# The dt projection of a hybrid decoder layer: plain fp32 with four 32-column blocks side by side, over an input summed on VectorE

## The chip, the core and the metric

The kernel runs on one core of a Trainium2 chip. The metric is the time of one execution on the device in microseconds (us). The engines are named as in the profile: PE is TensorE's matrix multiply and PEld its weight load, DVE is VectorE, ACT is ScalarE, POOL is GpSimd, and SP issues most of the transfers. Each engine takes its instructions in the order in which the program lists them.

## What is computed

One layer of a hybrid decoder is applied to 1024 prompt rows and to 64 sample rows (8 sequences of 8). Both go through one input projection, which is here the part that matters:

```python
h = _rmsnorm(x, norm_pre)
proj = jnp.einsum('bld,de->ble', h, w_in)
z, xbc, dt_raw, u, g, gates = jnp.split(proj, IN_OFFSETS, axis=-1)
...
dt = jax.nn.softplus(dt_raw.astype(F32) + dt_bias.astype(F32))
a = -jnp.exp(a_log.astype(F32))
y, new_ssm = _ssd(xs, dt, a, bm, cm, ssm_state.astype(F32))
```

`dt_raw` has one column for each of 16 heads. From dt follow the decays of a chunked scan (`_ssd`). The remaining columns of the projection go through a causal convolution, a pooling branch and gates, then through two branch projections and one output projection. All inputs and outputs are fp32.

## The kernel before

The 1088 rows lie along the free dimension as columns. The normalised input stands transposed in SBUF as a pair, `Hhi` and `Hlo`, each of 8 slices (k) of 128 partitions by 1088 columns: `Hhi` is the value rounded to the matmul's reduced fp32 type (fp32r) and `Hlo` the rest. Weights are split in the same way into `whi` and `wlo`. A 128-column piece of a projection is the work of `group3` (L143): for each of three column chunks (`CHUNKS`: 384, 384 and 320 columns), 8 slices times 3 products, `Hhi`*`whi`, `Hlo`*`whi` and `Hhi`*`wlo`.

The order of all work is written by hand. `main` is a list of matmul groups, one for each slot of the program; `at(slot, fn, key=...)` puts other work behind a slot's matmuls, sorted by key, and `at_pe` puts PE work ahead of them. Slots 0 to 5 are the groups of the first two convolution pieces, slots 6 to 8 those of the third (`cv[8]`), slot 9 is the dt projection (`DtStep.group`), and slot 10 the next convolution piece. Behind each convolution group come its evacuation from PSUM (`evac`, ACT, L335 to L343, one slot later, key 0), three multiply-adds of the convolution (`taps`, DVE, L349, two slots later, key 5), and a tanh on ACT (L356) with a product on DVE (`fin`, L357 and L360, three slots later, key 1). While convolution pieces run, ACT rounds the weights of the next piece (L94) and POOL takes the rest (L95).

`DtStep` computes dt. `load` fetches the 16 weight columns into `dst` and clears `dsw`, `conv` splits them into two column groups of `dsw`, so that one product gives the high and the low part of the weight in different output rows. `group` runs 3 chunks times 8 slices times 2 products (L388). `evac` copies 32 output rows to SBUF (L410), `tok` turns them by nine transposes (L416) so that rows become partitions, and `softplus` adds the two halves (L424) and takes the softplus (L426 to L437). `cums` (L441 to L444) makes the running sums by four matmuls two slots later. A scratch pool `z` of 13 tiles of 128 x 1088 is handed out by `zt()` and given back by `zfree()`.

Further on, the sample rows use matmuls of plain fp32 whose outputs are 32 partitions high, four side by side by `tile_position=(0, 32 * c)` (L752).

Of the kernel before, what the change touches and what calls it, by code (L numbers as in the profile page):

```python
# [9 lines left out]
F32 = mybir.dt.float32  # L10
F32R = mybir.dt.float32r
I32 = mybir.dt.int32
AF = mybir.ActivationFunctionType
ALU = mybir.AluOpType
# [5 lines left out]
NS = DB * DS  # L20
LT = LP + NS
# [4 lines left out]
C_Z, C_X, C_B, C_C, C_DT, C_U, C_G, C_GA, C_GB = 0, 1024, 2048, 2304, 2560, 2576, 3088, 3600, 4624  # L26
# [12 lines left out]
def hybrid_decoder_step(  # L39
# [6 lines left out]
    nc = tc.nc  # L46
# [11 lines left out]
    def nm(s):  # L58
        uid[0] += 1
        return f"{s}_{uid[0]}"  # L60
# [4 lines left out]
    def zt(shape=(128, LT), dt=F32):  # L65
        for s in big:
            if s.free:
                s.free -= 1
                t = s.pool.tile(list(shape), dt, tag=s.tag, name=nm(s.tag))
                owner[id(t)] = (s, t)  # L70
                return t
        raise AssertionError("no slot is free")

    def zfree(*ts):
        for t in ts:
            owner.pop(id(t))[0].free += 1
# [7 lines left out]
    def ct(shape, name, dt=F32):  # L84
        return cst.tile(shape, dt, name=name)

    def bank(tag):
        return px.tile([128, 512], F32, tag=tag, name=nm(tag))
# [4 lines left out]
    def split(hi, lo, src, eng=None):  # L93
        nc.scalar.copy(hi, src)  # L94
        (eng or nc.vector).tensor_tensor(lo, src, hi.bitcast(F32), op=ALU.subtract)  # L95
# [6 lines left out]
    def at(slot, fn, *args, key=1):  # L102
        post[slot].append((key, len(post[slot]), fn, args))

    def at_pe(slot, fn, *args, first=False):
        pe[slot].insert(0 if first else len(pe[slot]), (fn, args))
# [8 lines left out]
    class Slab:  # L115
# [8 lines left out]
        def conv(self, eng=None):  # L124
            self.hi = wp.tile([128, 8, 128], F32R, tag="whi", name=nm("whi"))
            self.lo = wp.tile([128, 8, 128], F32R, tag="wlo", name=nm("wlo"))
            n = self.kn
            split(self.hi[:, 0:n], self.lo[:, 0:n], self.raw[:, 0:n], eng)
# [23 lines left out]
    ident = ct([128, 128], "ident")  # L152
# [6 lines left out]
    Hhi = hpool.tile([128, KD, LT], F32R, name="Hhi")  # L159
    Hlo = hpool.tile([128, KD, LT], F32R, name="Hlo")  # L160
# [9 lines left out]
    s1 = s0_ctx.__enter__()  # L170
# [127 lines left out]
    class Conv:  # L298
# [15 lines left out]
        def group(self, c):  # L314
            t, box = group3(self.slab, c, hrhs, self.ch)
            at(t + 1, self.evac, c, box, key=0)
            at(t + 2, self.taps, c, key=5)
            at(t + 3, self.fin, c, key=1)
            return t
# [49 lines left out]

    class DtStep:  # L370
        def load(self):
            self.raw = s1.tile([128, 8, 16], F32, tag="dst", name="dst")
            nc.sync.dma_start(self.raw, w_in[0].rearrange("(k p) e -> p k e", p=128)[:, :, C_DT:C_DT + 16])
            self.w = s1.tile([128, 8, 128], F32R, tag="dsw", name="dsw")
            nc.gpsimd.memset(self.w.bitcast(F32), 0.0)

        def conv(self):
            split(self.w[:, :, 0:16], self.w[:, :, 16:32], self.raw, nc.gpsimd)

        def group(self):  # L380
            box = {}

            def emit():
                for c, (a, b) in enumerate(CHUNKS):
                    ps = box[c] = bank(("m0", "pyo", "pyo")[c])
                    for k in range(8):
                        for p, h in enumerate((Hhi, Hlo)):
                            nc.tensor.matmul(ps[:, 0:b - a], self.w[:, k], h[:, k, a:b], start=k == 0 and p == 0,  # L388
                                             stop=k == 7 and p == 1)

            main.append(emit)
            t = len(main) - 1
            at(t + 1, self.evac, box, key=0)
            at_pe(t + 3, self.tok)
            at(t + 3, self.softplus)
            at_pe(t + 5, self.cums)
            at(t + 5, self.cums_post)
            at_pe(t + 6, self.rowsT)
            at(t + 6, self.rows_post, key=4)
            at(t + 7, self.store)  # L400
            at(t + 22, common_a, key=6)
            at(t + 25, common_b, key=6)
            at(t + 26, common_c, key=6)

        def evac(self, box):
            self.dtr = zt((32, LT))
            self.tmp = zt((128, 5, 9, 16))
            nc.gpsimd.memset(self.tmp[64:128, 0, 8], 0.0)
            for c, (a, b) in enumerate(CHUNKS):
                nc.scalar.copy(self.dtr[:, a:b], box[c][0:32, 0:b - a])  # L410

        def tok(self):
            self.pd = bank("pst")
            for t in range(9):
                n = 128 if t < 8 else NS
                nc.tensor.transpose(self.pd[0:n, 32 * t:32 * t + 32], self.dtr[:, 128 * t:128 * t + n], ident[0:32, 0:32])  # L416
            zfree(self.dtr)

        def softplus(self):
            v, tt, u, e, r = (self.tmp[:, i] for i in range(5))  # L420
            self.adt = v
            for n, t0, m in ((128, 0, 8), (NS, 8, 1)):
                d = v[0:n, t0:t0 + m]
                nc.vector.tensor_reduce(d, self.pd[0:n, 32 * t0:32 * t0 + 32 * m].rearrange("p (t i h) -> p t h i", t=m, i=2),  # L424
                                        axis=mybir.AxisListType.X, op=ALU.add)
                nc.vector.tensor_tensor(d, d, bias_b[0:n].unsqueeze(1).to_broadcast([n, m, 16]), op=ALU.add)  # L426
            nc.scalar.activation(tt, v, AF.Abs)
            nc.scalar.activation(tt, tt, AF.Exp, scale=-1.0)
            nc.vector.tensor_scalar(u, tt, 1.0, None, op0=ALU.add)
            nc.vector.tensor_scalar(e, u, 1.0, None, op0=ALU.subtract)  # L430
            nc.vector.tensor_tensor(e, tt, e, op=ALU.subtract)
            nc.vector.reciprocal(r, u)
            nc.vector.tensor_tensor(e, e, r, op=ALU.mult)
            nc.scalar.activation(u, u, AF.Ln)
            nc.vector.tensor_tensor(e, e, u, op=ALU.add)
            nc.vector.scalar_tensor_tensor(dtv, v, 0.0, e, op0=ALU.max, op1=ALU.add)
            nc.vector.tensor_tensor(v, dtv, na.unsqueeze(1).to_broadcast([128, 9, 16]), op=ALU.mult)  # L437
# [732 lines left out]
    for slot, part in enumerate(plan.split("|")):  # L1170
        for w in part.split():
            fn, n = steps[w[0]], int(w[1])
# [9 lines left out]
    at(0, cv[8].slab.dma, key=5)  # L1182
    dts = DtStep()
    at(3, dts.load, key=5)
    at(6, dts.conv, key=5)
    at(2, hist_dma, key=5)
    at(5, zfree, npre, key=9)

# [67 lines left out]
    for j in range(8):  # L1256
        pr = Pair(j)
        pr.tx = p4 - 1 + j // 4 * 7
        t = p4 + 1 + 2 * j
# [250 lines left out]
```

## Time and profile before

| | us |
|---|---|
| median of 3 runs | 894.23 (893.12 to 894.34) |
| the profiled execution: its time | 894.35 |
| its span (first to last instruction) | 892.6 |
| PE busy | 879.9 (99%) |
| PEld busy | 843.7 (95%) |
| DVE busy | 551.2 (62%) |
| ACT busy | 348.8 (39%) |
| POOL busy | 217.4 (24%) |

The time lies 1.75 us above the span. A row of the timeline gives start and duration of an instruction, or of several equal ones in a row, in us from the span's start, and in brackets how long the engine was idle ahead of it and what ended that. Matmuls overlap, so their durations add up to more than the time they take; what one takes in a stream is the distance between starts. A plain fp32 matmul has two rows, a matmul on fp32r operands one.

### The profile page before, as it was taken

How to read it: one execution, taken by the hardware profiler on the slowest of the kernel's cores; microseconds unless marked ns; L12 is line 12 of the kernel's file. 1: busy time of each engine (PE TensorE's matmuls, PEld its weight loads, DVE VectorE, ACT ScalarE, POOL GpSimd, SP SyncE). 2: the span in 40 equal slices, each digit the busy share in tenths (PEclk: the TensorE clock that was granted, in tenths of full speed). 3: DMA queues.
4: the chain of work that ended last, by engine and by line, in shares of the span. 5: the costliest groups of instructions: out<-in, count | busy, mean ns of one | idle time of the engine just before them, and what ended most of it. 6: DMA issues, size and time to landing. Idle time of an engine off the chain costs nothing.

```text
span 892.6 us, 14398 instructions
## 1 busy us (share of the span) xinstructions
PE 879.9 (99%) x5558; PEld 843.7 (95%) x5558; DVE 551.2 (62%) x999; ACT 348.8 (39%) x770; POOL 217.4 (24%) x297
## 2 busy tenths in 40 slices
PE   7999999999999999999999999999999999999997
PEld 5999999999999999999999999999999999988886
DVE  6776796989667765457746554357356627963322
ACT  6645565656375543345333141112333224331111
POOL 6332264756465652121100000000000000001101
PEclk9999999999999999999999999999999999999999
DMA  8010233342345335453311124433111123722322
GB/s 275 9 48 24 77 95 97 99 128 71 103 129 156 105 96 164 127 160 101 95 49 36 54 84 149 143 114 99 34 49 51 31 79 115 264 74 71 100 99 85
DMA packets 110322, 87.97 MB, mean 99 GB/s; under 512 B 8474, under 2 KB 97550, under 8 KB 110253
## 3 DMA queue, kind: packets, MB, share of 16 engines
q1 hardware_dynamic: 110109, 86.98, 32.5%
q8 instruction: 44, 0.72, 0.3%
q14 instruction: 25, 0.20, 0.1%
q10 hardware_dynamic: 144, 0.07, 0.0%
HBM read 69.46 MB, written 17.56 MB: 97 GB/s over the span
## 4 chain that ended last, share of the span: by engine, by line
PE 93%; DVE 1%; ACT 1%; POOL 1%; issue 0%; DVEq 0%; POOLq 0%; ACTq 0%
PE m L143 54%; PE pyo L143 16%; PE m L1399 3%; PE pyo L1399 3%; PE xb L1399 2%; PE pst L1399 2%; PE pyo L575 2%; PE pyo L582 2%; PE pst L586 1%; PE xb L711 1%; PE xb L542 1%; PE pyo L388 1%; DVE r L841 1%; PE pyo L752 1%; PE pst L759 0%
## 5 line engine op out<-in xcount | busy, mean ns | idle before, releaser
L143 PE MATMUL m<-Hhi,whi 128*128 128x384 f32 (+3 forms) x872 | 289.0, 331 | 0.0
L143 PE MATMUL m<-Hhi,wlo 128*128 128x384 f32 (+3 forms) x872 | 285.4, 327 | 0.0
L143 PE MATMUL m<-Hlo,whi 128*128 128x384 f32 (+3 forms) x872 | 285.3, 327 | 0.0
L143 PEld LDWEIGHTS m<-Hhi,whi 128*128 128x128 f32 x872 | 164.6, 189 | 0.6
L143 PEld LDWEIGHTS m<-Hlo,whi 128*128 128x128 f32 x872 | 164.6, 189 | 0.3
L143 PEld LDWEIGHTS m<-Hhi,wlo 128*128 128x128 f32 x872 | 164.4, 189 | 0.3
L349 DVE SCALAR_TENSOR_TENSOR r<-r,par,r 128x384 f32<-128x384 f32 (+3 forms) x108 | 94.6, 876 | 2.6
L94 ACT CAST whi<-raw 128x1024 fp32r<-128x1024 f32 (+1 forms) x67 | 59.8, 892 | 91.4 <-PE m L143 53.6
L95 DVE TENSOR_TENSOR wlo<-raw,whi 128x512 fp32r<-128x512 f32 (+1 forms) x46 | 43.4, 944 | 65.2 <-ACT whi L94 65.1
L95 POOL TENSOR_TENSOR wlo<-raw,whi 128x1024 fp32r<-128x1024 f32 x21 | 51.6, 2457 | 40.9 <-ACT whi L94 40.9
L143 PE MATMUL pyo<-Hhi,whi 128*128 128x384 f32 (+1 forms) x184 | 59.8, 325 | 0.0
L143 PE MATMUL pyo<-Hhi,wlo 128*128 128x384 f32 (+1 forms) x184 | 59.7, 325 | 0.0
L143 PE MATMUL pyo<-Hlo,whi 128*128 128x384 f32 (+1 forms) x184 | 59.7, 324 | 0.0
L143 PE MATMUL m<-z,whi 128*128 128x384 f32 (+1 forms) x217 | 54.0, 327 | 0.0
L143 PE MATMUL pyo<-z,whi 128*128 128x384 f32 (+1 forms) x191 | 47.7, 327 | 0.0
L568 POOL TENSOR_TENSOR sa<-sa,cb 128x512 f32<-128x512 f32 x28 | 39.8, 1441 | 3.7 <-ACT sa L564 3.7
L143 PEld LDWEIGHTS m<-z,whi 128*128 128x128 f32 x217 | 38.4, 188 | 0.0
L143 PE MATMUL m<-z,wlo 128*128 128x384 f32 (+1 forms) x115 | 37.6, 327 | 0.0
L563 ACT ACTIVATE sa<-sa,acm 128x128 f32<-128x128 f32 x112 | 35.6, 389 | 0.0
L609 DVE SCALAR_TENSOR_TENSOR z<-z,dsk,se 128x128 f32<-128x128 f32 x56 | 34.8, 660 | 1.0
L1434 POOL TENSOR_SCALAR t<-t 128x1 f32<-128x1 f32 (+1 forms) x9 | 2.5, 276 | 133.7 <-ACT q L1431 133.7
L143 PEld LDWEIGHTS pyo<-Hlo,whi 128*128 128x128 f32 x184 | 34.6, 188 | 0.0
(386 smaller groups left out, 1608.5 us busy)
## 6 DMA issues: line engine op xcount, KB each, us to landing
raw<-in_w_in_dram SPq DMA_DIRECT2D x43, 512.0 KB, 4.0
z<-in_x_prompt_dram SPq DMA_DIRECT2D x15, 512.0 KB, 4.5
sa<-dscr SPq DMA_DIRECT2D x28, 256.0 KB, 4.4
z<-spill SPq DMA_DIRECT2D x11, 544.0 KB, 5.1
raw<-in_w_branch_a_dram SPq DMA_DIRECT2D x16, 256.0 KB, 2.8
r<-in_w_out_dram SPq DMA_DIRECT2D x16, 256.0 KB, 4.4
se<-dscr SPq DMA_DIRECT2D x56, 64.0 KB, 3.8
out_dram<-q SPq DMA_DIRECT2D x14, 256.0 KB, 2.1
```

The source lines that it names most:

```text
L94: nc.scalar.copy(hi, src)
L95: (eng or nc.vector).tensor_tensor(lo, src, hi.bitcast(F32), op=ALU.subtract)
L143: nc.tensor.matmul(ps[:, 0:b - a], slab.w(k, p), rhs(k, p)[:, a:b], start=k == 0 and p == 0, stop=k == slab.kn - 1 and p == 2)
L349: nc.vector.scalar_tensor_tensor(A, R[:, k:k + w], cw(k, i), A, op0=ALU.mult, op1=ALU.add)
L388: nc.tensor.matmul(ps[:, 0:b - a], self.w[:, k], h[:, k, a:b], start=k == 0 and p == 0, stop=k == 7 and p == 1)
L542: nc.tensor.transpose(p[:, 128 * i:128 * i + 128], X[2 * self.u + i][:, self.cols], ident)
L563: nc.scalar.activation(A[:, h], A[:, h], AF.Relu, bias=acm[:, self.c, hh:hh + 1], scale=-1.0)
L568: nc.gpsimd.tensor_tensor(A, A, CBs[self.c, self.g].unsqueeze(1).to_broadcast([128, 4, 128]), op=ALU.mult)
L575: nc.tensor.matmul(py[64 * q:64 * q + 64, 128 * i:128 * i + 128], s.x0[:, 2 * i + q], s.A[:, 2 * i + q], start=True, stop=True)
L582: nc.tensor.matmul(py[:, 256 + 128 * i:384 + 128 * i], hs[:, 128 * i:128 * i + 128], Ct[self.g][:, self.cols], start=True, stop=True)
L609: nc.vector.scalar_tensor_tensor(xv, xv, dsk[:, j:j + 1], self.E[:, i] if self.c else py[:, 128 * i:128 * i + 128], op0=ALU.mult, op1=ALU.add)
L1399: nc.tensor.matmul(box["ps"][:, 0:b - a], lh, rh[k][:, a:b], start=kk == 0 and i == 0, stop=kk == 7 and rh is Wlo)
```

## The change

The high and low parts of the input are added on DVE, one slice at a time, into eight full fp32 tiles (`whole`, placed in slots 5 to 8, two in each slot, with key 9). The weight is kept in plain fp32, padded to 32 columns, and no longer split. The dt projection then runs as 24 plain fp32 matmuls: in each chunk, slices 0 to 3 go to the output partitions 0, 32, 64 and 96, and slices 4 to 7 are accumulated on them. The four partial sums are evacuated as 128 rows, transposed as full 128-row tiles into three PSUM banks, and added by the reduction in `softplus`, which now adds four parts and is made of three instructions.

```diff
--- before.py
+++ after.py
@@ -369,13 +369,15 @@
 
     class DtStep:
         def load(self):
-            self.raw = s1.tile([128, 8, 16], F32, tag="dst", name="dst")
-            nc.sync.dma_start(self.raw, w_in[0].rearrange("(k p) e -> p k e", p=128)[:, :, C_DT:C_DT + 16])
-            self.w = s1.tile([128, 8, 128], F32R, tag="dsw", name="dsw")
-            nc.gpsimd.memset(self.w.bitcast(F32), 0.0)
-
-        def conv(self):
-            split(self.w[:, :, 0:16], self.w[:, :, 16:32], self.raw, nc.gpsimd)
+            self.w = s1.tile([128, 8, 32], F32, tag="dsw", name="dsw")
+            nc.gpsimd.memset(self.w, 0.0)
+            nc.sync.dma_start(self.w[:, :, 0:16], w_in[0].rearrange("(k p) e -> p k e", p=128)[:, :, C_DT:C_DT + 16])
+
+        def whole(self, k):
+            if k == 0:
+                self.h = []
+            self.h.append(zt())
+            nc.vector.tensor_tensor(self.h[k], Hhi[:, k].bitcast(F32), Hlo[:, k].bitcast(F32), op=ALU.add)
 
         def group(self):
             box = {}
@@ -383,10 +385,12 @@
             def emit():
                 for c, (a, b) in enumerate(CHUNKS):
                     ps = box[c] = bank(("m0", "pyo", "pyo")[c])
-                    for k in range(8):
-                        for p, h in enumerate((Hhi, Hlo)):
-                            nc.tensor.matmul(ps[:, 0:b - a], self.w[:, k], h[:, k, a:b], start=k == 0 and p == 0,
-                                             stop=k == 7 and p == 1)
+                    for r in range(2):
+                        for g in range(4):
+                            k = 4 * r + g
+                            nc.tensor.matmul(ps[32 * g:32 * g + 32, 0:b - a], self.w[:, k], self.h[k][:, a:b], start=r == 0,
+                                             stop=r == 1, tile_position=(0, 32 * g))
+                zfree(*self.h)
 
             main.append(emit)
             t = len(main) - 1
@@ -403,26 +407,29 @@
             at(t + 26, common_c, key=6)
 
         def evac(self, box):
-            self.dtr = zt((32, LT))
+            self.dtr = zt()
             self.tmp = zt((128, 5, 9, 16))
             nc.gpsimd.memset(self.tmp[64:128, 0, 8], 0.0)
             for c, (a, b) in enumerate(CHUNKS):
-                nc.scalar.copy(self.dtr[:, a:b], box[c][0:32, 0:b - a])
+                nc.scalar.copy(self.dtr[:, a:b], box[c][:, 0:b - a])
 
         def tok(self):
-            self.pd = bank("pst")
+            self.pd = [bank("xb"), bank("xb"), bank("pst")]
             for t in range(9):
                 n = 128 if t < 8 else NS
-                nc.tensor.transpose(self.pd[0:n, 32 * t:32 * t + 32], self.dtr[:, 128 * t:128 * t + n], ident[0:32, 0:32])
+                q = 128 * (t % 4)
+                nc.tensor.transpose(self.pd[t // 4][0:n, q:q + 128], self.dtr[:, 128 * t:128 * t + n], ident)
             zfree(self.dtr)
 
         def softplus(self):
             v, tt, u, e, r = (self.tmp[:, i] for i in range(5))
             self.adt = v
+            for n, t0, m in ((128, 0, 4), (128, 4, 4), (NS, 8, 1)):
+                d = v[0:n, t0:t0 + m]
+                nc.vector.tensor_reduce(d, self.pd[t0 // 4][0:n, 0:128 * m].rearrange("p (t g x) -> p t x g", t=m, g=4)[:, :, 0:16],
+                                        axis=mybir.AxisListType.X, op=ALU.add)
             for n, t0, m in ((128, 0, 8), (NS, 8, 1)):
                 d = v[0:n, t0:t0 + m]
-                nc.vector.tensor_reduce(d, self.pd[0:n, 32 * t0:32 * t0 + 32 * m].rearrange("p (t i h) -> p t h i", t=m, i=2),
-                                        axis=mybir.AxisListType.X, op=ALU.add)
                 nc.vector.tensor_tensor(d, d, bias_b[0:n].unsqueeze(1).to_broadcast([n, m, 16]), op=ALU.add)
             nc.scalar.activation(tt, v, AF.Abs)
             nc.scalar.activation(tt, tt, AF.Exp, scale=-1.0)
@@ -1182,7 +1189,8 @@
     at(0, cv[8].slab.dma, key=5)
     dts = DtStep()
     at(3, dts.load, key=5)
-    at(6, dts.conv, key=5)
+    for k in range(8):
+        at(5 + k // 2, dts.whole, k, key=9)
     at(2, hist_dma, key=5)
     at(5, zfree, npre, key=9)
```

On DVE the instructions of slots 5 to 7 stood as follows before: products (L357, L360) and multiply-adds (L349, three in a row) of the convolution, on tiles `r` (scratch) and `z` (results).

```order
L349 SCALAR_TENSOR_TENSOR r_543<-r_540,par,r_543 128x384 x3
L357 SCALAR_TENSOR_TENSOR z_390<-r_649,r_543 128x384
L349 SCALAR_TENSOR_TENSOR r_607<-r_600,par,r_607 128x472 x3
L357 SCALAR_TENSOR_TENSOR z_349<-r_694,r_607 128x384
L360 SCALAR_TENSOR_TENSOR z_349<-r_694,r_607 128x64
L349 SCALAR_TENSOR_TENSOR r_647<-r_640,par,r_647 128x472 x3
```

In the same place of the changed kernel, up to the sums of slices 4 and 5:

```order
L349 SCALAR_TENSOR_TENSOR r_542<-r_539,par,r_542 128x384 x3
L380 TENSOR_TENSOR z_614<-Hhi,Hlo 128x1088
L380 TENSOR_TENSOR z_616<-Hhi,Hlo 128x1088
L357 SCALAR_TENSOR_TENSOR z_390<-r_652,r_542 128x384
L349 SCALAR_TENSOR_TENSOR r_606<-r_599,par,r_606 128x472 x3
L380 TENSOR_TENSOR z_664<-Hhi,Hlo 128x1088
L380 TENSOR_TENSOR z_666<-Hhi,Hlo 128x1088
L357 SCALAR_TENSOR_TENSOR z_349<-r_699,r_606 128x384
L360 SCALAR_TENSOR_TENSOR z_349<-r_699,r_606 128x64
L349 SCALAR_TENSOR_TENSOR r_650<-r_643,par,r_650 128x472 x3
L380 TENSOR_TENSOR z_706<-Hhi,Hlo 128x1088
L380 TENSOR_TENSOR z_708<-Hhi,Hlo 128x1088
```

Two sums stand behind each slot's multiply-adds and ahead of the next slot's product; the last two (slices 6 and 7) stand behind the next three multiply-adds on 128x384.

On PE the dt projection of the first chunk stood behind the third convolution piece (its last products on L143) as alternating products of `Hhi` and `Hlo`.

```order
L143 MATMUL m_115_701<-Hlo,whi_548 128x320
L143 MATMUL m_115_701<-Hhi,wlo_549 128x320
L388 MATMUL m_119_738<-Hhi,dsw 128x384
L388 MATMUL m_119_738<-Hlo,dsw 128x384
L388 MATMUL m_119_738<-Hhi,dsw 128x384
L388 MATMUL m_119_738<-Hlo,dsw 128x384
```

In the changed kernel the first chunk reads all eight sums, and the second chunk (`pyo`) begins with the first sum again:

```order
L143 MATMUL m_121_710<-Hlo,whi_547 128x320
L143 MATMUL m_121_710<-Hhi,wlo_548 128x320
L391 MATMUL m_127_751<-z_614,dsw 32x384
L391 MATMUL m_127_751<-z_616,dsw 32x384
L391 MATMUL m_127_751<-z_664,dsw 32x384
L391 MATMUL m_127_751<-z_666,dsw 32x384
L391 MATMUL m_127_751<-z_706,dsw 32x384
L391 MATMUL m_127_751<-z_708,dsw 32x384
L391 MATMUL m_127_751<-z_747,dsw 32x384
L391 MATMUL m_127_751<-z_749,dsw 32x384
L391 MATMUL pyo_760<-z_614,dsw 32x384
```

PE's place for the projection is the same; its operands are now the tiles that DVE writes in slots 5 to 8.

## Rows read from the trace of the kernel before

**Rows 1.** The page's chain that ended last, shares by engine.

```profile
PE 93%; DVE 1%; ACT 1%; POOL 1%; issue 0%; DVEq 0%; POOLq 0%; ACTq 0%
```

**Rows 2.** Waits of PE, whole span: total us, times, longest; all there are.

```profile
PE m L1160 <- DMA hst<-in_norm_pre_dram: 2.5, 1, 2.5
PE xb L224 <- DVE xn L210: 2.4, 1, 2.4
PE pst L224 <- DVE xn L210: 1.5, 2, 1.2
```

**Rows 3.** Timeline of PE: the dt projection's first matmul and what follows its last.

```profile
60.88 0.34 PE L388 MATMUL m<-Hhi,dsw 128*128 128x384 f32 x1
...
68.89 0.34 PE L143 MATMUL m<-Hhi,whi 128*128 128x384 f32 x1
```

**Rows 4.** Timeline of DVE behind slots 5 to 8.

```profile
48.16 0.56 DVE L357 SCALAR_TENSOR_TENSOR z<-r,r 128x384 f32<-128x384 f32 x1 [1.49 <-ACT r L356]
48.64 1.92 DVE L349 SCALAR_TENSOR_TENSOR r<-r,par,r 128x384 f32<-128x384 f32 x3
51.15 0.56 DVE L357 SCALAR_TENSOR_TENSOR z<-r,r 128x384 f32<-128x384 f32 x1 [0.59 <-ACT r L356]
51.62 4.28 DVE L349 SCALAR_TENSOR_TENSOR r<-r,par,r 128x472 f32<-128x472 f32 x3
56.70 0.56 DVE L357 SCALAR_TENSOR_TENSOR z<-r,r 128x384 f32<-128x384 f32 x1 [0.80 <-ACT r L356]
...
57.31 2.19 DVE L349 SCALAR_TENSOR_TENSOR r<-r,par,r 128x472 f32<-128x472 f32 x3
60.17 0.56 DVE L357 SCALAR_TENSOR_TENSOR z<-r,r 128x384 f32<-128x384 f32 x1 [0.67 <-ACT r L356]
...
60.79 1.92 DVE L349 SCALAR_TENSOR_TENSOR r<-r,par,r 128x384 f32<-128x384 f32 x3
```

**Rows 5.** DVE's groups by shape, a two-operand instruction on 1024 columns: busy us, mean ns.

```profile
L95 DVE TENSOR_TENSOR wlo<-raw,whi 128x1024 fp32r<-128x1024 f32 x22 | 26.9, 1223 | 41.7 <-ACT whi L94 41.7
```

**Rows 6.** Timeline of POOL: its splits of weights near the dt projection.

```profile
52.13 2.44 POOL L95 TENSOR_TENSOR wlo<-raw,whi 128x1024 fp32r<-128x1024 f32 x1 [2.05 <-ACT whi L94]
...
71.00 2.39 POOL L95 TENSOR_TENSOR wlo<-raw,whi 128x1024 fp32r<-128x1024 f32 x1 [8.59 <-ACT whi L94]
```

**Rows 7.** Timeline of PE: plain fp32 matmuls, full width (L441) and in 32-column blocks (L752).

```profile
85.73 0.38 PE L441 MATMUL pst<-z,tri 128*128 128x128 f32 x2
...
359.71 0.34 PE L143 MATMUL m<-Hhi,wlo 128*128 128x384 f32 x1
359.98 0.64 PE L752 MATMUL pyo<-hT,hst 128*32 128x128 f32 x16
360.56 0.73 PE L759 MATMUL pst<-bk,z 96*128 96x512 f32 x2
```

**Rows 8.** Line L752: count, duration in ns (min/median/max) of one row.

```profile
L752 PE MATMUL pyo<-hT,hst x96: 272/273/298, 360.0 to 433.6; 128*32 128x128 f32 x96
```

**Rows 9.** Timeline of PE: transposes of 32 rows (L416) and of 128 rows (L711).

```profile
77.31 0.71 PE L416 MATMUL pst<-ident,z 32*128 32x32 f32 x9
...
361.13 1.04 PE L711 MATMUL xb<-ident,h 128*128 128x128 f32 x8
```

**Rows 10.** Timeline of DVE: the reduction and the last step of softplus.

```profile
78.06 0.42 DVE L424 TENSOR_REDUCE z<-pst 128x128 f32<-128x256 f32 x1 [2.55 <-PE pst L416]
...
82.87 0.31 DVE L437 TENSOR_TENSOR z<-dtv,m 128x144 f32<-128x144 f32 x1
```

**Rows 11.** PE idle early (timeline), then stretches: length, PE busy, granted clock, DMA share.

```profile
16.32 0.63 PE L224 MATMUL xb<-ident,xn 128*128 128x128 f32 x4 [2.43 <-DVE xn L210]
...
16.00:18.00 2.00, 1.68 (x12) 0.82 1.05 314
18.00:20.00 2.00, 2.00 (x12) 0.50 1.17 255
20.00:21.30 1.30, 1.30 (x10) 0.74 0.13 34
```

## The prediction

> **What bounds the kernel now.** The first view is the page's chain of work that ended last: PE holds 93% of it [rows 1]. The second is the list of PE's waits over the whole span [rows 2]. It has four waits, for the first transfer and for the normalisation of the input, all at lines of the opening. After the transposes of the input PE waits for nobody. So the kernel is bound by PE almost throughout, and near the dt projection each microsecond that PE gains or loses should show in the end: no other engine has a wait there that would swallow it. PE's timeline gives the place [rows 3]: the dt projection starts at 60.88 and the next convolution piece at 68.89, so the stage takes 8.01 us for 48 matmuls. The last view is DVE's timeline up to that place [rows 4], because the changed matmuls read what DVE writes there. The reader is to see how little room it has: between 50.56 (48.64 + 1.92) and 62.71 (60.79 + 1.92) it is idle for 0.59 + 0.80 + 0.67 = 2.06 us.
>
> **The matmuls.** A plain fp32 matmul has two rows. At full width two rows on 128 columns (L441) span 0.38 us; the second alone lasts 0.27 [rows 7, 8], so they start 0.11 apart. In 32-column blocks (L752) 16 rows span 0.64 [rows 7], the last lasts 0.27, so the 16 starts lie within 0.37; four rows side by side then cost 0.37 / 3 = 0.12, nearly what one costs at full width. The blocks do run side by side. Here the columns are 384, 384 and 320 instead of 128: three times as much, 0.33 (from 0.11) to 0.37 (from 0.12) for four rows, and 0.28 to 0.31 for 320 columns. A chunk is 8 matmuls, 16 rows, four such steps: 1.3 to 1.5, 1.3 to 1.5 and 1.1 to 1.2, in all 3.8 to 4.1 (I take 3.95). Entering and leaving costs about 0.1 each: L752 starts 0.27 after the row ahead of it where a stream has 0.17 [rows 7]. So the matmuls alone go from 8.01 to 4.15, a gain of 3.9 us, if their operands are there.
>
> A rule of the Trainium skill speaks against full packing: "TensorE: Matmul & The Clock Gate", Part 3 (measured speedup), gives four row blocks a speedup of 3.07 and three column blocks 2.38, not 4 and 3. By 3.07 the 3.95 would be 5.1 (an estimate from that page). The rows above stand closer to 4, and I keep them.
>
> **The sums.** The operands are eight new DVE instructions of 1088 columns on two SBUF operands. The nearest row is a two-operand instruction on 1024 columns, 1.22 us [rows 5]. At the difference between this and the 384-column product (0.56 [rows 4]), 0.66 us for 640 columns, 64 more columns add 0.07: 1.29. The next instruction starts about 0.08 before the end of one (51.15 + 0.56 against 51.62 [rows 4]), so each takes 1.21 of DVE, the eight 9.7 us. They wait for nothing themselves, `Hhi` and `Hlo` being complete long before; but DVE runs in order, and they stand behind the multiply-adds of slots 5 to 8. The last two stand behind the multiply-adds that end at 62.71 in the trace of before, which is already 1.8 us after the projection began. Six sums stand ahead of these. If DVE's 2.06 us of idle time are all used (the tanh for which it waited is then done earlier than DVE arrives), the last sum ends at 62.71 + 8 x 1.21 - 2.06 = 70.33. I round to 70.35 for PE. On the way the second sum should be done near 53.0, the fourth near 60, the sixth near 65.2.
>
> One thing moves this by about half a microsecond either way. POOL's split at 52.13 holds DVE up: the multiply-adds beside it took 4.28 us where three of the same shape take 2.19 [rows 4, 6]. In the changed kernel the second sum (51.8 to 53.1) is running when POOL wants to start. If POOL waits for it, the block ends later than before; if not, the sum hides part of it. The bounds are 69.8 and 70.9. The split of `dsw` on POOL and its rounding on ACT go away; both engines have idle time there, so that gives nothing on the path.
>
> **The wait that follows.** PE takes its queue in order, so behind the waiting matmul stands everything else of PE, from the next convolution piece on, and behind that all other engines. In the first chunk the first four matmuls run at about 61, and the others trickle in with their sums. The one on the last slice starts at 70.35 and takes two rows of 384 columns, 0.65, alone: 71.0. The other two chunks then run without a wait: 1.4 + 1.15, and 0.1 to leave, 73.65. The next piece started at 68.89 before; it is 4.75 us late. At the bounds: 69.8 + 0.65 + 2.4 + 0.05 = 72.9, 4.0 late, and 70.9 + 0.7 + 2.7 + 0.1 = 74.4, 5.5 late.
>
> **The rest.** ACT copies the same number of columns, on 128 rows instead of 32, with no more columns per row: nothing. The nine transposes grow from 32 rows to 128. Before, nine span 0.71 and the last lasts about 0.2: 0.06 apart; eight of 128 rows span 1.04 and the last lasts 0.27: 0.11 apart [rows 9]. Nine times 0.05 is 0.4 us, on PE's path. The reduction becomes two instructions of 256 elements and a small one: one more of 0.42 [rows 10]. It is hidden: softplus ended at 83.18 (82.87 + 0.31) and PE's running sums started at 85.73 [rows 7, 10], 2.5 us later, of which 0.4 goes. If that cover were gone, it would cost 0.42. The weight's transfer now waits for the clearing of its tile on POOL; both stand some 25 us ahead of use.
>
> **The clock.** PE is nearly idle from 61.6 to 70.35, four short matmuls apart. The trace of before has an idle stretch of 2.43 us ahead of 16.32 [rows 11], after which the granted clock falls to 0.50, the lower level of 1.2 GHz: by the three stretches 0.18 x 2.0 + 0.50 x 2.0 + 0.26 x 1.3 = 1.7 us of work are lost between 16 and 21.3, while PE was busy. The wait here is longer, so I expect a fall, but when it begins is open: part of it may lie in the wait itself, and a new one may start just as PE resumes. I take 1.4 for it, with bounds 0 and 2.6.
>
> The same page of the Trainium skill (Part 1, the clock gate) says that an idle PE goes back to half its clock and gets the full clock only after sustained work; the trace of before agrees, with the 0.50 just named.
>
> **The sum.** 4.75 + 0.4 + 1.4 = 6.55 us later. On the profiled execution's 894.35 this gives 900.9; that execution lies 0.12 above the median of the runs, so I predict 900.8. The bounds: 4.0 + 0.3 + 0 = 4.3, that is 898.5, and 5.5 + 0.45 + 2.6 = 8.55, that is 902.8.
>
> **Rivals.**
> The first ends on the other side: the sums are ready in time, and the change gains 3.9 - 0.4 = 3.5, 890.7. For it speaks that DVE is only 62% busy over the span. But the average says nothing here: the room in front of PE's start is 2.06 us for 9.7 us of work. The point that decides: PE breaks even if the last sum is ready at 70.35 - 5.15 = 65.2, clock aside. That wants 0.57 us for each sum, less than half of what 1024 columns cost. I give it 0.04.
>
> The second: DVE does the sums at about twice the rate of that row, 0.6 each. Then the last sum is there at 65.5, the delay is 0.3 us and the time 894.5, no change. Against it, all 22 instructions of that row have two SBUF operands in 4-byte types as here, and take 1.22. 0.03.
>
> The third: at 384 columns, each from another place in SBUF, the blocks don't run side by side as they do at 128. Each matmul then costs 2 x 0.33 (0.28), the two free chunks 8 x 0.66 + 8 x 0.56 = 9.8 instead of 2.55, and the time is 908. Nothing in the trace shows wide blocks; the rows at 128 columns are clean. 0.04.
>
> The fourth is the forecast without a fall of the clock: 4.75 + 0.4, 899.4. 0.2. The forecast itself, with a fall, has 0.65. The remaining 0.04 are for something later on that I don't see, such as a buffer that comes free late; where the new order makes an engine wait for DVE, several microseconds are to spare (the evacuation of the third piece, for instance, now waits for DVE until about 66, and PE needs it at 73.65).
>
> **How the numbers follow.** A measurement of this kernel can tell about 0.2%, 1.8 us, from no change. The range 898.0 to 903.2 takes in the bounds of the forecast with and without the fall, and some 0.85 of the chance. Slower by over 0.2%: 0.65 + 0.2 + 0.04 + 0.03 = 0.92; faster: 0.04; the same: 0.04.
>
> **What would show it.** PE should have its longest wait of the run at L391, for DVE's L380, some 8 us in four or five pieces, where before it had none. The eight L380 should last 1.29 each, and the last end near 70.35. The second and third chunk should show four rows of L391 each 0.33 to 0.37. From the end of the projection on the two timelines should run in parallel. If DVE's sums were short, or their waits ended by 65, or four rows took over 0.6, the prediction is wrong at that step; if PE's clock stays at full, the time is near 899.4.

## The result, and the profile after

The changed kernel takes 901.19 us (median of 5 runs, 899.91 to 901.27) against 893.16 before on the same chip: a ratio of 1.0078, 95% interval 1.0067 to 1.0089. It is slower, as predicted, and the predicted 900.8 (898.0 to 903.2) holds it. The runs of most kernels here fall on two levels 1.1 to 1.5 us apart, whose profiles differ in the opening (PE's first matmul on 448 columns starts at 37.8 to 38.4 in the upper and at 36.7 to 36.9 in the lower), so differences below are taken between equal levels: 893.1 to 899.9 and 894.3 to 901.2, both times +6.8 to +6.9. The profile after has the shorter opening, that of before the longer one: the same multiply-adds begin at 47.30 and at 48.64 [rows 4], so 1.34 is added to a time of after to set it beside one of before.

The page's chain that ended last, of the changed kernel (by engine):

```profile
PE 90%; DVE 4%; ACT 1%; POOL 1%; issue 0%; DVEq 0%; POOLq 0%; ACTq 0%
```

The waits of PE, changed kernel (total us, times, longest):

```profile
PE m L391 <- DVE z L380: 4.0, 2, 2.2
PE m L1167 <- DMA hst<-in_norm_pre_dram: 2.3, 1, 2.3
...
PE xb L224 <- DVE xn L210: 0.9, 1, 0.9
PE m L391 <- ACT r L335: 0.4, 1, 0.4
```

DVE has come into the chain, where it had 1% [rows 1], and PE's largest total of waiting is no longer in the opening [rows 2] but at L391, the blocks, for L380, the sums; the longest single wait, 2.3, is still in the opening. This list counts less than PE lost there, because a wait can lie inside a row's duration. Who waited for L380 (us, times), with PE's weight loads (PEld):

```profile
  PEld m L391: 8.1, 4
  PE m L391: 4.0, 2
```

The 8.1 us in four pieces are the wait that the prediction described (some 8 us in four or five). DVE's timeline, changed kernel, answering to [rows 4]:

```profile
47.30 1.92 DVE L349 SCALAR_TENSOR_TENSOR r<-r,par,r 128x384 f32<-128x384 f32 x3
49.13 2.49 DVE L380 TENSOR_TENSOR z<-Hhi,Hlo 128x1088 f32<-128x1088 f32 x2
51.54 2.76 DVE L357 SCALAR_TENSOR_TENSOR z<-r,r 128x384 f32<-128x384 f32 x1
54.22 2.19 DVE L349 SCALAR_TENSOR_TENSOR r<-r,par,r 128x472 f32<-128x472 f32 x3
56.33 2.49 DVE L380 TENSOR_TENSOR z<-Hhi,Hlo 128x1088 f32<-128x1088 f32 x2
...
61.45 2.48 DVE L380 TENSOR_TENSOR z<-Hhi,Hlo 128x1088 f32<-128x1088 f32 x2
...
64.46 1.92 DVE L349 SCALAR_TENSOR_TENSOR r<-r,par,r 128x384 f32<-128x384 f32 x3
66.29 2.50 DVE L380 TENSOR_TENSOR z<-Hhi,Hlo 128x1088 f32<-128x1088 f32 x2
```

No row has an idle gap ahead of it: the 2.06 us of room are used up. The pairs end at 51.62, 58.82, 63.93 and 68.79. PE's timeline, changed kernel, answering to [rows 3]; the last row is the next convolution piece:

```profile
60.06 0.85 PE L391 MATMUL m<-z,dsw 128*32 128x384 f32 x8 [0.36 <-ACT r L335]
62.78 2.69 PE L391 MATMUL m<-z,dsw 128*32 128x384 f32 x4 [1.87 <-DVE z L380]
67.64 2.05 PE L391 MATMUL m<-z,dsw 128*32 128x384 f32 x3 [2.17 <-DVE z L380]
68.85 0.92 PE L391 MATMUL pyo<-z,dsw 128*32 128x384 f32 x3
69.48 0.85 PE L391 MATMUL m<-z,dsw 128*32 128x384 f32 x1
69.49 4.77 PE L391 MATMUL pyo<-z,dsw 128*32 128x384 f32 x29
...
74.19 0.45 PE L143 MATMUL m<-Hhi,whi 128*128 128x384 f32 x1
```

The first four slices run at once (8 rows from 60.06), then PE stands still for one sum after the other. A row of several instructions can hold a wait: the four rows at 62.78 are two slices whose sums come 1.2 us apart. The stage takes 14.13 us (60.06 to 74.19) where it took 8.01 [rows 3]. Stretches of the changed kernel (length, busy us and count of PE, PEld, DVE, ACT and POOL, then the granted clock, DMA share, GB/s):

```profile
61.00:63.00 2.00, 0.21 (x1) 0.14 (x2) 2.00 (x3) 0.60 (x1) 0.00 (x0) 1.00 0.00 0
63.00:66.00 3.00, 2.48 (x4) 0.18 (x2) 2.93 (x6) 0.67 (x3) 0.95 (x4) 0.52 0.01 3
66.00:68.00 2.00, 0.36 (x1) 0.18 (x2) 2.00 (x3) 0.93 (x2) 0.55 (x2) 0.50 0.00 0
68.00:73.00 5.00, 5.00 (x30) 1.95 (x32) 3.03 (x5) 0.55 (x2) 0.00 (x0) 0.50 0.01 3
73.00:74.00 1.00, 1.00 (x10) 0.29 (x2) 0.00 (x0) 0.41 (x1) 0.00 (x0) 0.82 0.00 0
```

The clock falls to its lower level (0.50, 1.2 GHz) after PE has stood nearly idle from 61 to 63, and stays there through 68 to 73, when PE is busy again: the whole tail of the projection runs at half speed. Four rows side by side then start 0.64 behind the four ahead of them (68.85, 69.49), above the 0.6 that the prediction named as a sign against it; at the full clock it is 0.33, as the kernel without sums shows below.

Last the transposes (L421), answering to [rows 9]: first what followed them before, then the changed kernel, each on PE's timeline.

```profile
77.95 0.42 PE L143 MATMUL m<-Hhi,whi 128*128 128x320 f32 x1
```

```profile
82.65 1.04 PE L421 MATMUL xb<-ident,z 128*128 128x128 f32 x8
83.52 0.27 PE L421 MATMUL pst<-ident,z 128*64 128x128 f32 x1
83.55 0.39 PE L143 MATMUL m<-Hhi,whi 128*128 128x320 f32 x1
```

They take 0.90 of PE where they took 0.64.

### The profile page after: what moved, and what is told of

Read it like the earlier page. It is cut to its first block, busy times and chain, and to the rows that moved or that the text cites. A ratio compares the mean times of both kernels' runs of the same rounds, so it can differ in the third digit from the quotient of the medians.

```text
span 898.2 us, 14405 instructions
## 1 busy us (share of the span) xinstructions
PE 882.9 (98%) x5558; PEld 839.0 (93%) x5558; DVE 561.2 (62%) x1008; ACT 348.8 (39%) x769; POOL 218.2 (24%) x296
## 4 chain that ended last, share of the span: by engine, by line
PE 90%; DVE 4%; ACT 1%; POOL 1%; issue 0%; DVEq 0%; POOLq 0%; ACTq 0%
PE m L143 52%; PE pyo L143 16%; PE m L1407 3%; PE pyo L1407 3%; PE xb L1407 2%; PE pst L1407 2%; PE pyo L582 2%; PE pyo L589 2%; PE pst L593 1%; DVE z L380 1%; DVE r L349 1%; PE xb L718 1%; PE xb L549 1%; DVE r L848 1%; PE pyo L759 1%
## 5 line engine op out<-in xcount | busy, mean ns | idle before, releaser
L143 PE MATMUL m<-Hhi,whi 128*128 128x384 f32 (+3 forms) x872 | 288.4, 331 | 0.0
L143 PE MATMUL m<-Hhi,wlo 128*128 128x384 f32 (+3 forms) x872 | 284.8, 327 | 0.0
L143 PE MATMUL m<-Hlo,whi 128*128 128x384 f32 (+3 forms) x872 | 284.6, 326 | 0.0
L143 PEld LDWEIGHTS m<-Hhi,whi 128*128 128x128 f32 x872 | 163.8, 188 | 1.0 <-issue 0.5
L143 PEld LDWEIGHTS m<-Hlo,whi 128*128 128x128 f32 x872 | 163.9, 188 | 0.3
L143 PEld LDWEIGHTS m<-Hhi,wlo 128*128 128x128 f32 x872 | 163.7, 188 | 0.2
L349 DVE SCALAR_TENSOR_TENSOR r<-r,par,r 128x384 f32<-128x384 f32 (+3 forms) x108 | 92.5, 856 | 2.6
L143 PE MATMUL pyo<-Hhi,whi 128*128 128x384 f32 (+1 forms) x184 | 59.8, 325 | 0.0
L143 PE MATMUL pyo<-Hhi,wlo 128*128 128x384 f32 (+1 forms) x184 | 59.7, 325 | 0.0
L143 PE MATMUL pyo<-Hlo,whi 128*128 128x384 f32 (+1 forms) x184 | 59.7, 324 | 0.0
L143 PE MATMUL m<-z,whi 128*128 128x384 f32 (+1 forms) x217 | 54.1, 327 | 0.0
L143 PE MATMUL pyo<-z,whi 128*128 128x384 f32 (+1 forms) x191 | 47.7, 327 | 0.0
L143 PEld LDWEIGHTS m<-z,whi 128*128 128x128 f32 x217 | 38.3, 188 | 0.0
L143 PE MATMUL m<-z,wlo 128*128 128x384 f32 (+1 forms) x115 | 37.6, 327 | 0.0
L143 PEld LDWEIGHTS pyo<-Hlo,whi 128*128 128x128 f32 x184 | 34.5, 188 | 0.0
```

Of the source, the lines that this page charges most:

```text
L143: nc.tensor.matmul(ps[:, 0:b - a], slab.w(k, p), rhs(k, p)[:, a:b], start=k == 0 and p == 0, stop=k == slab.kn - 1 and p == 2)
L349: nc.vector.scalar_tensor_tensor(A, R[:, k:k + w], cw(k, i), A, op0=ALU.mult, op1=ALU.add)
```

## The experiments

All ratios are set against the kernel before, run in the same series on the same chip. The last column is the kernel's fastest run (before: 892.7 to 893.1).

| kernel | median us | ratio, 95% interval | fastest run, us |
|---|---|---|---|
| as changed | 901.19 | 1.0078 (1.0067 to 1.0089) | 899.9 |
| sums unread | 895.12 | 1.0013 (1.0004 to 1.0021) | 893.9 |
| no sums | 890.36 | 0.9958 (0.9945 to 0.9970) | 888.9 |
| one group later | 894.53 | 1.0015 (1.0006 to 1.0024) | 894.3 |
| filled wait | 899.53 | 1.0063 (1.0051 to 1.0076) | 898.0 |
| half the sums | 891.51 | 0.9985 (0.9976 to 0.9994) | 891.4 |
| two groups later | 895.09 | 1.0022 (1.0011 to 1.0033) | 893.8 |
| slice by slice | 896.57 | 1.0042 (1.0030 to 1.0055) | 896.4 |
| half the sums, later | 892.41 | 0.9992 (0.9984 to 1.0001) | 892.2 |
| two groups later, no sums | 890.18 | 0.9953 (0.9939 to 0.9966) | 889.1 |
| two groups later, spread | 899.68 | 1.0061 (1.0048 to 1.0073) | 897.9 |
| sums three a slot | 896.52 | 1.0032 (1.0019 to 1.0044) | 895.3 |
| six sums | 892.91 | 0.9984 (0.9976 to 0.9993) | 891.8 |

**The sums alone (sums unread).** To the kernel before:

```
+    for k in range(8):
+        at(5 + k // 2, dts.whole, k, key=9)
```

> The kernel before with the eight DVE sums of Hhi and Hlo added at the places that the change gives them; nobody reads them, and the old 48 matmuls stand, so the output is the reference's. Theory (only TensorE's wait for the sums costs): the sums delay nothing else that TensorE waits for, and the time is that of before, 893.2, to within +0.5. Rival (the sums crowd DVE and GpSimd out, and the evacuations and the GpSimd splits beside them come late by themselves): +3 to +7, 896 to 900.

Measured: +0.9 (893.0 to 893.9, 894.3 to 895.2). The waits of PE in that kernel have one new row:

```profile
PE m L395 <- POOL r L334: 0.7, 1, 0.7
```

So DVE's extra 9.7 us cost 0.9, a little over the theory's 0.5, and 0.7 of it is a wait for an evacuation that comes late; the rest of the loss of 6.9 is not crowding.

**The matmuls alone (no sums).** To the changed kernel:

```
-                            nc.tensor.matmul(ps[...], self.w[:, k], self.h[k][:, a:b], ...)
+                            nc.tensor.matmul(ps[...], self.w[:, k], Hhi[:, k, a:b].bitcast(F32), ...)
...
-    for k in range(8):
-        at(5 + k // 2, dts.whole, k, key=9)
```

> The changed kernel without the eight sums: the blocks read Hhi alone, in plain fp32, so the Hlo part of dt's input is left out. Theory: with nothing to wait for, the matmuls' gain comes out, 8.0 - 4.15 = 3.9 less 0.3 for the wider transposes: 893.2 - 3.6 = 889.6 (889 to 890.2). Rival (four blocks do not run side by side at 384 columns): the 24 plain matmuls take about 15 us where the 48 took 8, and the time is 900.

Measured 888.9 to 890.4: 4.0 faster than before (893.0 to 889.0, 894.3 to 890.4), where the theory had 3.6. PE's timeline of that kernel:

```profile
59.57 1.50 PE L391 MATMUL m<-Hhi,dsw 128*32 128x384 f32 x16
60.89 2.55 PE L391 MATMUL pyo<-Hhi,dsw 128*32 128x384 f32 x32
63.37 0.44 PE L143 MATMUL m<-Hhi,whi 128*128 128x384 f32 x1
```

48 rows, no wait, 3.80 us in all (59.57 to 63.37); the first chunk's 16 rows take 1.32, four rows 0.33. The blocks run side by side at 384 columns, which rules the prediction's third rival out. The sums, with what they bring, cost the changed kernel 899.9 - 889.0 = 10.9 us.

**One group later.** To the changed kernel:

```
     for i in (8, 10, 2, 3):
         for c in range(3):
             cv[i].group(c)
-        if i == 8:
-            dts.group()
+            if i == 10 and c == 0:
+                dts.group()
```

> The changed kernel with the projection one convolution group later in TensorE's order (some 4.2 us), the sums where they were. Theory (the loss is the wait for the last sum plus the low clock that follows the wait): the wait shrinks by about 4 us, so 901.2 - 4 = 897.2; if the clock then stays at 1.00 for longer, another 1 to 2 us less, 895.5. Rival (DVE falls behind as a whole, so that whatever stands there waits): the later group's own input is late too and nothing is gained, 900 to 901.2.

Measured 894.3 to 895.6: 5.6 to 5.7 less than the changed kernel (899.9 to 894.3, 901.2 to 895.5), the second figure of the theory, in which the clock stays up as well. Stretches of that kernel, columns as above:

```profile
64.00:68.00 4.00, 2.35 (x17) 0.73 (x16) 3.93 (x7) 2.54 (x5) 1.42 (x5) 1.00 0.01 2
68.00:72.00 4.00, 3.63 (x36) 1.26 (x34) 3.98 (x3) 0.46 (x1) 3.24 (x3) 1.00 0.00 0
```

The clock stays at 1.00, and the tail behind the last sum, the same 33 rows as in the changed kernel, takes 3.21 us on PE's timeline of that kernel (68.86 to 72.07) where there it takes 5.34 (68.85 to 74.19). That is the price of the half clock: 2.13.

```profile
68.86 0.52 PE L391 MATMUL pyo<-z,dsw 128*32 128x384 f32 x3
69.20 0.49 PE L391 MATMUL m<-z,dsw 128*32 128x384 f32 x1
69.21 2.85 PE L391 MATMUL pyo<-z,dsw 128*32 128x384 f32 x29
72.07 0.45 PE L143 MATMUL m<-Hhi,whi 128*128 128x384 f32 x1
```

**The clock alone (filled wait).** To the changed kernel:

```
+    FILL = {4: 9, 5: 3, 6: 15, 7: 3}
...
+                            if c == 0 and k in FILL:
+                                fb = bank("xb")
+                                for f in range(FILL[k]):
+                                    nc.tensor.matmul(fb[:, 0:384], cv[8].slab.w(0, 0), Hhi[:, f % 8, 0:384], start=True, stop=True)
```

> The changed kernel with 30 matmuls of 384 columns in fp32r, into a bank that nobody reads, ahead of slices 4 to 7 of the first chunk, so that TensorE has work while it waits for the sums. Theory (2 us or so of the loss are matmuls at the half clock that follows the wait): the granted clock stays at 1.00 and the next convolution group begins 2 to 2.5 us earlier, 898.7 to 899.2 against 901.2. Rival (the half clock costs nothing, the sums alone set the end): no change, 901.2, or slower by what the filler overruns the wait.

Measured 898.0 and 899.5, 1.9 and 1.7 less than 899.9 and 901.2. The last sums on DVE's timeline of that kernel, and the next piece on PE's:

```profile
67.95 2.50 DVE L382 TENSOR_TENSOR z<-Hhi,Hlo 128x1088 f32<-128x1088 f32 x2
74.10 0.45 PE L143 MATMUL m<-Hhi,whi 128*128 128x384 f32 x1
```

The last sum ends at 70.45 and the next piece begins 3.65 later, where the changed kernel needs 5.40 (68.79 to 74.19); 0.5 of the expected gain went to filler that overran the wait (slice 7 starts at 70.97). The stretch that holds the tail, in that kernel:

```profile
70.00:73.00 3.00, 3.00 (x32) 1.47 (x35) 2.68 (x5) 0.48 (x1) 0.00 (x0) 1.00 0.00 0
```

Thirty useless matmuls make the kernel faster, because they keep the clock up. The rival (the half clock costs nothing) falls.

**The tail's order (slice by slice).** To the changed kernel:

```
+                for r in range(2):
+                    for g in range(4):
+                        k = 4 * r + g
+                        for c, (a, b) in enumerate(CHUNKS):
+                            nc.tensor.matmul(box[c][...], self.w[:, k], self.h[k][:, a:b], ...)
```

> The changed kernel with its 24 matmuls in another order: slice by slice, each slice for all three chunks (three banks at once), where the change goes chunk by chunk. The sums and the wait for the last of them are the same; but behind the last sum there are 3 matmuls and not 17. Theory (the tail that waits behind the last sum, at the half clock, is part of the loss): the tail of 5.3 us becomes 1 to 2 us, and the time 901.2 - 3.8 = 897.4 (896.5 to 898.5). Rival (only the end of the last sum counts, or the blocks one at a time take the tail back): 900 to 901.2.

Measured 896.4 to 897.9, 3.4 less. PE's timeline of that kernel, whose last sum ends at 70.16 (its opening is the longer one):

```profile
70.21 0.51 PE L392 MATMUL m<-z,dsw 128*32 128x384 f32 x1
70.33 0.43 PE L392 MATMUL pyo<-z,dsw 128*32 128x320 f32 x1
70.56 0.49 PE L392 MATMUL m<-z,dsw 128*32 128x384 f32 x1
70.60 1.63 PE L392 MATMUL pyo<-z,dsw 128*32 128x320 f32 x5
72.16 0.44 PE L143 MATMUL m<-Hhi,whi 128*128 128x384 f32 x1
```

Behind the last sum stand 1.95 us in place of 5.34. Its PE has more to do while it waits, and the clock stays at 1.00 from 61 on. So the 3.4 are not the order alone: at the full clock the old order needs 3.21 (one group later), so 2.13 of the difference is the clock and 1.26 the shorter tail. The loss is the wait for the last sum plus whatever is queued behind it. Here too is what a slice costs without others beside it: the three chunks of slice 6 take 1.87 (its first row starts at 69.01, and the row behind its last one at 70.88), 15.0 for eight, against 3.80 side by side: 3.9 times.

**Fewer sums (half the sums; six sums).** In the first, slices 0 to 3 are summed and slices 4 to 7 are read as `Hhi` and `Hlo`, three rounds of four blocks:

```
+                src = self.h[0:4] + [x[:, k].bitcast(F32) for x in (Hhi, Hlo) for k in range(4, 8)]
...
-    for k in range(8):
+    for k in range(4):
         at(5 + k // 2, dts.whole, k, key=9)
```

> The changed kernel with only the sums of slices 0 to 3 (the ones that end by 58.8 on the changed kernel's profile, ahead of the projection at 60.06); the blocks of slices 4 to 7 read Hhi and then Hlo, in plain fp32 as well, so that there are three rounds of four blocks a chunk and not two. The output is the reference's. Theory: 36 matmuls take 1.5 x 4.15 = 6.2 in place of 8.0, nothing waits, half the sums crowd by half of what the unread ones cost (0.9 / 2): 893.3 - 1.8 + 0.3 + 0.4 = 892.2 (891.6 to 893). Rival (the sums cost by their number, waited for or not; all eight cost some 11 beside the kernel without them): half of 11 is 5.5, so 897.

Measured 891.4 and 892.7: 1.6 faster than before (893.0, 894.3), and far from the 897 of a cost by the number of sums. PE waits 0.4 for an evacuation and for no sum. In the second, slices 0 to 5 are summed, and the blocks of slices 4 and 5 stand behind all others:

```
+                seq += [(c, 2 * (c == 1) + k - 4, k, self.h[k]) for c in range(3) for k in (4, 5)]
...
-    for k in range(8):
+    for k in range(6):
```

> A candidate: the sums of slices 0 to 5, slices 6 and 7 read as Hhi and Hlo; first two rounds of four blocks for each chunk, and the matmuls of slices 4 and 5 for all three chunks behind them, two chunks side by side; the place is that of the change. The output is the reference's. Theory: slices 4 and 5 are read some 4 us behind the projection's start (60.1), when their sums (end 63.9) are ready; the matmuls take 2 x 1.85 + 1.2 = 4.9 in place of the 5.5 of the kernel with half the sums, and two more sums crowd by 0.2: 891.1 (890.7 to 892) against 891.5. Rival (the sums of slices 4 and 5 stand in DVE's queue ahead of a convolution's steps and hold an evacuation back): 892.5 or more.

Measured 891.8 and 893.0: no sum is waited for either, and the projection takes 5.23 us (60.04 to 65.27) in place of 5.62 (60.07 to 65.69), but the time is 0.4 above that of half the sums, not below it. On PE's timeline its lead is 0.44 at the transposes (73.70 against 74.14) and gone at 88.09 against 88.10, where PE waits for DVE's copy of the running sums; where the other 0.4 goes stays open.

**Two groups later.** The projection behind the second group of `cv[10]`, weights in another buffer, store and readers for the samples re-timed:

```
-            self.w = s1.tile([128, 8, 32], F32, tag="dsw", name="dsw")
+            self.w = zt((128, 8, 32))
...
-            at(t + 7, self.store)
+            at(t + 6, self.store, key=5)
...
+            if i == 10 and c == 1:
+                dts.group()
```

> The changed kernel, all eight sums, with the projection two convolution groups later (behind the second group of the Conv object 10), its weights in another buffer, its store one slot earlier against the projection and the steps that read the results for the samples left where they stood. Theory: the sums end at 68.8 and the projection starts no earlier, so that TensorE waits for none; left are the gain of the kernel without sums (4.0) and the crowding of the unread ones (0.9): 893.3 - 4.0 + 0.9 = 890.2 (889.5 to 891). Rival (the wait moves to whoever needs the projection's results two groups earlier): the loads of the decay factors come late for the first unit, and the time is that of the kernel one group later or worse, 894.5 and above.

Measured 893.8 to 896.6: the theory's 890.2 is far off, and the rival's 894.5 and above is near. In its profile PE waits for no sum, but for an evacuation (waits of PE, then ACT, DVE and POOL on the timeline):

```profile
PE m L391 <- ACT r L335: 2.4, 1, 2.4
```

```profile
72.77 0.48 ACT L335 COPY r<-m 128x384 f32<-128x384 f32 x1 [3.64 <-DVE z L357]
67.55 2.50 DVE L380 TENSOR_TENSOR z<-Hhi,Hlo 128x1088 f32<-128x1088 f32 x2
69.97 2.71 DVE L357 SCALAR_TENSOR_TENSOR z<-r,r 128x384 f32<-128x384 f32 x1
69.21 3.06 POOL L95 TENSOR_TENSOR wlo<-raw,whi 128x1024 fp32r<-128x1024 f32 x1 [1.51 <-ACT whi L94]
```

The last pair of sums holds L357 back to 69.97; there it meets POOL's split and takes 2.71 instead of 0.55; the evacuation L335 needs the buffer that L357 frees; and PE needs the bank that L335 empties. The rival named another cause, loads that come late because the results are wanted earlier, and PE's waits do not show it. To tell the place from the sums:

```
-                            nc.tensor.matmul(ps[...], self.w[:, k], self.h[k][:, a:b], ...)
+                            nc.tensor.matmul(ps[...], self.w[:, k], Hhi[:, k, a:b].bitcast(F32), ...)
...
-    for k in range(8):
-        at(5 + k // 2, dts.whole, k, key=9)
```

> The kernel with the projection two groups later, without its eight sums: the blocks read Hhi alone, so the Hlo part of dt's input is left out. Theory (the sums, in DVE's queue ahead of a convolution's own steps, made TensorE wait 2.4 for an evacuation; the place itself costs nothing): the time is that of the kernel without sums at the first place, 889.0 to 890.4, to within 0.7. Rival (the place is bad by itself: the loads, the store and the readers of the projection's results come late): 892 or more, most of the loss stays.

Measured 889.1 and 890.3, the times of the kernel without sums at the first place: the place costs nothing, the sums in DVE's queue cost 4.7 there. Of these, 3.9 are four waits of PE for evacuations (2.4, 0.7, 0.4, 0.4) that the kernel without sums does not have. Half of the sums, one group later (the edits of the two kernels together, the weights in another buffer):

> The sums of slices 0 to 3 alone, slices 4 to 7 in two plain fp32 rounds, as in the kernel with half the sums, and the projection one convolution group later. Theory: with half the sums TensorE has nothing to wait for at either place, so the two places give the same time to within 0.7: 892.2. Rival (the place itself costs, by what is evacuated beside it): 893.5 or more.

Measured 892.2 and 893.5: 0.8 above half the sums at the first place, just outside the theory's 0.7; 0.4 of it is a wait of PE for an evacuation of a gate (L934) that the first place does not have.

**Where the sums stand (spread; three a slot).**

```
-        at(5 + k // 2, dts.whole, k, key=9)
+        at((5, 5, 6, 7, 7, 8, 9, 10)[k], dts.whole, k, key=9)
```

> The kernel with the projection two groups later, all eight sums, spread over slots 5 to 10 (two, one, one, two, one, one) and not in pairs over 5 to 8. Theory (a pair of 2.5 ahead of a convolution's steps holds its evacuation back, one of 1.25 is half hidden): TensorE's wait for the evacuation falls by 1.2 or more and nothing waits for the last sum, 893.8 - 1.2 to 893.8 - 3: 890.8 to 892.6 on the lower of this kernel's two levels of time. Rival (what counts is DVE's whole load in the stretch, wherever the sums stand): unchanged, 893.5 to 895, or worse where the last sum is now the late one.

Measured 897.9 to 900.0, 4 slower: the wait for the evacuation is gone, but the last sum now stands behind later multiply-adds and ends at 76.66 (DVE's timeline), 7 us after PE began the projection at 69.59, and the granted clock is 0.50 from 75 to 80. That is the last case that the rival allowed for. PE's waits, that kernel:

```profile
PE m L391 <- DVE z L380: 4.8, 2, 2.5
```

The other way round, at the place of the change:

```
-        at(5 + k // 2, dts.whole, k, key=9)
+        at(5 + k // 3, dts.whole, k, key=9)
```

> The changed kernel with the sums three a slot, in slots 5 to 7 and not 5 to 8; the projection where the change puts it. Theory (the end of the last sum sets TensorE's wait): one convolution chunk's DVE steps, 2.5, no longer stand ahead of the last sum, which ends at about 66.3 in place of 68.8, and the time falls by 2 to 2.5: 898.7 to 899.2 against 901.2. Rival (DVE's load as a whole sets it, so that what the sums gain the convolutions lose): no change, 900.7 to 901.2.

Measured 895.3 to 898.5; by the ratios 4.1 less than the changed kernel. In the profiled execution (897.14, the shorter opening as in the profile after) the last sum ends at 66.33, 2.46 earlier, and the next piece begins 2.77 earlier (71.42), a little over the theory's 2.5. The clock falls here too (0.50 from 64 to 70), and the tail takes 5.03 (66.39 to 71.42). Other runs gain up to 1.9 beyond that. The mean granted clock is 0.995 in the profiled run, 0.996 and 0.997 in two of 896.5 and 0.997 in the fastest (895.3), and 0.001 of the span is 0.9 us, so the clock is the likely reason, but no trace of those runs shows it. Its waits show what was traded:

```profile
PE m L391 <- ACT r L335: 2.6, 1, 2.6
PE m L391 <- DVE z L380: 0.9, 1, 0.9
```

## Why the prediction was right

**The matmuls** went from 8.01 to 3.80 where nothing waits (no sums), predicted 4.15 (3.95 without entering and leaving). The row chosen for four blocks side by side was the right one: 0.33 for 384 columns was predicted as 0.33 to 0.37. The 3.07 that the Trainium skill, "TensorE: Matmul & The Clock Gate", Part 3 (measured speedup), gives for four row blocks is not what this stream of four column blocks shows: here it is 3.9.

**The sums** last 1.28 to 1.30, predicted 1.29. Set beside before (+1.34) the pairs end at 52.96, 60.16, 65.27 and 70.13; predicted were 53.0, 60, 65.2 and 70.35. DVE did run through its 2.06 us of idle time, and the error is 0.2. What POOL's split costs DVE also came out nearly equal, 2.21 in L357 (2.76 for 0.55) where it was 2.09 in the multiply-adds before (4.28 for 2.19); this the prediction had left open.

**The wait that follows.** At full clock the tail behind the last sum takes 3.21; predicted were 0.65 + 2.55 + 0.1 = 3.3. The point of break-even and the rival in which the sums are ready were thus judged rightly: the last sum came 5 us after 65.2.

**The clock** fell, as the likeliest case had it, but cost 2.13 and not 1.4. This term was too small: 1.4 allowed for a part of the fall inside the wait, and in fact the lower level held through the whole busy tail up to 73. That an idle PE goes back to half its clock and gets the full one only after work (the Trainium skill, "TensorE: Matmul & The Clock Gate", Part 1) agrees with the stretches, 1.00 at 61 to 63, 0.50 at 68 to 73, and 1.00 again behind 74. But the length of a wait did not settle whether the clock fell. PE's wait of 2.43 us in the opening is followed by the 0.82, 0.50 and 0.74 of [rows 11] in the trace of before, and by 1.00 from 16 to 22 in that of the kernel without sums, which has the same wait; and the wait of 2.4 in the kernel two groups later left the clock at 1.00. So the single fall from which the prediction took its size was a weak ground, and the fourth rival rightly kept a chance. In the changed kernel the fall came in every run: the mean granted clock is 0.991 to 0.993, where it is 0.997 to 0.999 before.

**The rest.** The transposes cost 0.26, predicted 0.4. The longer reduction stayed hidden: softplus ends at 88.63 (L444, 88.32 + 0.31) and the running sums begin at 91.31.

**The sum.** The next piece begins at 74.19 + 1.34 = 75.53 instead of 68.89, 6.64 late (predicted 4.75 + 1.4 = 6.15), and 0.26 more come with the transposes: 6.9, as measured. Predicted were 6.55; the clock's 0.7 too little is partly made good by a last sum 0.2 earlier, a tail 0.1 shorter and transposes 0.14 cheaper. That the total is within 0.4 is in part luck.

**What it left out.** The evacuations: the prediction gave them microseconds to spare, and at this place that is right (0.4 us of PE's waits). But there PE stood waiting for the sums anyway. In three kernels that keep all eight sums and in which that wait is gone or short, one for an evacuation appears: 0.7 us (sums unread), 2.4 (two groups later) and 2.6 (three a slot).

## What to carry to other kernels

A cheaper matmul that wants an operand made first is paid for on the engine that makes it: compare the work with the idle time of that engine ahead of the piece, not with its average (62% busy here, and 2 us of room for 9.7 us). Where the operand is late, price the wait, then what is queued behind it, then the clock that falls meanwhile; another order of the matmuls, which also kept the clock up, was worth 3.4 us. And take as much of the change as fits the room: four sums of eight, the other slices read in two parts, give 891.4 at the fastest, 1.6 us under the kernel before, where all eight give 899.9; the gain is just told from none (ratio 0.9976 to 0.9994).

## What the runs showed of the hardware beyond that

POOL and DVE hold each other up. In the changed kernel POOL's split begins while a sum runs and takes 3.09 where it took 2.44 [rows 6]; DVE's L357 behind that sum then takes 2.76 instead of 0.55 and ends 0.4 after the split. POOL's timeline, changed kernel:

```profile
50.80 3.09 POOL L95 TENSOR_TENSOR wlo<-raw,whi 128x1024 fp32r<-128x1024 f32 x1 [2.04 <-ACT whi L94]
```

The sum ended at 51.62; from there to the split's end at 53.89 are 2.27, about one split, as if POOL had waited for the sum and L357 then for the split. "SBUF — State Buffer" of the Trainium skill (SBUF: two separate sides) says that a DVE instruction with two SBUF inputs and one of GpSimd that reads SBUF exclude each other for the whole instruction, whichever starts first; the rows agree, both ways.
